# Two of the four block sums of an input projection's pair, moved from a VectorE add to an accumulating DMA

## The chip, the cores and the metric

The kernel runs on one core of a Trainium2 chip. The metric is the device time of one execution in microseconds; the profile is one execution of the same program, taken by the hardware profiler. TensorE does the matrix products, VectorE (DVE in the profile) and ScalarE (ACT) prepare their operands, GpSimd (POOL) does next to nothing before the change, and SyncE (SP) issues nearly all transfers.

## The reference, cut to what matters

One layer of an encoder over 256 tokens of width 4096, all in float32. The two matrices, 4096 x 13312 and 4096 x 4096, are read from HBM once.

```python
h = layer_norm(x, emb_ln_g, emb_ln_b)
p = h @ w_in                    # 256 x 4096 times 4096 x 13312
c_b, c_c, c_h, c_z, a_q, a_k, a_v, a_z = split(p)
y_conv = c_b * centred_short_conv(c_c * c_h, conv_w) * silu(c_z)
y_attn = banded_window_attention(a_q, a_k, a_v, sink) * silu(a_z)
y = concatenate([y_conv, y_attn]) @ w_out
out = layer_norm(2 ** 0.25 * h + y, ln_g, ln_b)
```

## The kernel before

**Steps.** The input projection is cut into 26 chunks of 512 output columns: k, v, then four times (gate z, query q), then four times (c, h, z, b) of the convolution. A chunk is made of steps, which are numbered through from 0; TensorE works them off in order. A single step (a letter `s` in the tables `ORDERS` and `OUT_ORDERS`) is a 1 MB piece of weights, four blocks of 128 rows by 512 columns, and 24 matmuls of 512 columns. A pair step (`S`) covers two such row blocks (512 KB) with a seven-product scheme in the manner of Strassen: it forms sums of quarter blocks, and 21 matmuls of 256 columns take the place of 24. All chunks after k and v have the order `sSsSSsSsSSs`: five singles and six pairs. The input projection has 24 x 6 = 144 pairs, kind `pair`; the output projection has 16 more, kind `opair`.

**A pair's blocks.** A weight buffer is a tile of 128 x 2048 float32, eight blocks of 256 columns. The load fills blocks 0 to 3 (b12, b22, b11, b21). `sums` then makes four more on VectorE: blocks 4 and 5 are blocks 1 and 2 plus block 0, in one instruction of 512 columns (L178); block 6 is block 5 plus block 1 (L179); block 7 is block 6 plus block 3 (L180). Seven blocks, 1 to 7, go on.

**Two halves.** Each step's weights are split into a high part, a copy rounded to float32r on ScalarE (`split_hi`, L197, tile `whi`), and a low part, the difference, on VectorE (`split_lo`, L201, tile `wlo`). TensorE takes three products per operand pair: high times high, high times low, low times high.

**What sets the order.** The order is written out by hand. While TensorE works step j, ScalarE is told to split step j+3, then come the pieces of attention or convolution that are due at j, then `loads(j)` on SP's queue, `sums(j+4)` on VectorE, and `split_lo(j+3)` on VectorE:

```python
        mm_pair(j) if kind == "pair" else mm(j)
        split_hi(j + 3)
...
        loads(j)
        sums(j + 4)
        split_lo(j + 3)
```

Every engine runs its list strictly in order, so the low part of step j+3 stands behind the sums of step j+4.

**The weight buffers.** A load goes into the buffer whose last user is oldest, and it waits until that user's low part is done. There are three buffers `w0` to `w2` and up to three further ones in tiles that are free at the time (`extra`): through most of the attention one more (`w6`), and from the convolution on three more. Between, while the tile of `w6` holds a chunk's sums, there are only the three, which the main loop writes as follows; z0 is 126, the first step of the convolution's first gate chunk, so this holds from step 108 to step 132:

```python
        if j == z0 - 18:
            extra.clear()
        if j == z0 + 6:
            extra.insert(0, (pw, "w6"))
```

With n buffers, the load of step k waits for the low part of step k-n.

Of the kernel before, what the change touches and what calls it, by code (L numbers as in the profile page):

```python
# [11 lines left out]
ALU = mybir.AluOpType  # L12
AX = mybir.AxisListType

P = 128
# [25 lines left out]
HW = W // 2  # L41
# [48 lines left out]
ALL_PAIRS = [u[1:] for u in IN_STEPS + OUT_STEPS if u[0] in ("pair", "opair")]  # L90
# [4 lines left out]
def encoder_kernel(ctx: ExitStack, tc: tile.TileContext, x, emb_g, emb_b, wi, ws, conv_w, sink, wo, ln_g, ln_b, out):  # L95
    nc = tc.nc
# [14 lines left out]
    steps = IN_STEPS + OUT_STEPS  # L111
# [12 lines left out]
    def w_bufs(j):  # L124

        bs = [(wpool, f"w{k}") for k in range(N_W)] + (extra if j < N_IN else [])
        if j >= N_IN and R is not None:
            late = j > in_R[0][0]
            bs += [(None, name) for last, name in in_R if j <= last and late == (name == "R2")]
        last_user = lambda b: max(u for c, u in user.items() if c == b or b[1] == "R2" and c[0] is None) if (  # L130
            b in user or b[1] == "R2") else -1
        return min((last_user(b), k) for k, b in enumerate(bs)), bs

    def load(j, to=None):
        kind, a, b = steps[j]
        if to is None:
            (_, k), bs = w_bufs(j)
            pool, name = bs[k]
            user[bs[k]] = j
            if pool is None:  # L140
                to = raw[j] = {"R0": R[:, 0, D // 2:D], "R1": R[:, 1, D // 2:D], "R2": R[:, :, 3 * D // 4:D]}[name]
            else:
                to = raw[j] = pool.tile([P, PIECE], F32, name=name, bufs=1)
        src = wi[IN_PIECES.index((a, b))] if kind == "in" else wo[OUT_PIECES.index((a, b))] if kind == "out" else None
        if len(to.shape) == 3:
            if is_pair(j):
                nc.sync.dma_start(out=to[:, 0, :], in_=ws[ALL_PAIRS.index((a, b))])
            else:
                nc.sync.dma_start(out=to, in_=src.rearrange("p (i n) -> p i n", i=2))
        elif is_pair(j):  # L150
            nc.sync.dma_start(out=to[:, 0:4 * HW], in_=ws[ALL_PAIRS.index((a, b))])
        else:
            nc.sync.dma_start(out=to, in_=src)

    def loads(j):

        nonlocal nxt
        while nxt < len(steps) and nxt <= j + 7:
            (u, _), bs = w_bufs(nxt)
            if u > j + (2 if len(bs) > N_W else 3):  # L160
                break
            load(nxt)
            nxt += 1

    def sums(j):

        if j >= len(steps) or not is_pair(j):
            return
        if len(raw[j].shape) == 3:
            r0, r1 = (raw[j][:, i, :].rearrange("p (b w) -> p b w", w=HW) for i in range(2))  # L170
            r = lambda k: (r1 if k >= 4 else r0)[:, k % 4, :]
            s01 = r1[:, 0:2, :]
            b12, b22 = r0[:, 0:1, :], r0[:, 1:3, :]
        else:
            t = raw[j].rearrange("p (b w) -> p b w", w=HW)
            r = lambda k: t[:, k, :]
            s01, b12, b22 = t[:, 4:6, :], t[:, 0:1, :], t[:, 1:3, :]
        nc.vector.tensor_tensor(s01, b22, b12.to_broadcast([P, 2, HW]), op=ALU.add)  # L178
        nc.vector.tensor_tensor(r(6), r(5), r(1), op=ALU.add)  # L179
        nc.vector.tensor_tensor(r(7), r(6), r(3), op=ALU.add)  # L180

# [99 lines left out]
    with tc.tile_pool(name="pro", bufs=1) as pro:  # L281
# [13 lines left out]
        nc.sync.dma_start(out=g_c, in_=emb_g)  # L295
        nc.sync.dma_start(out=b_c, in_=emb_b)
        load(0, first[0])
        load(1, first[1])
        x_load(1)
        for j in range(2, 4):  # L300
# [34 lines left out]
        pair = {}  # L335
# [426 lines left out]
    for j in range(n_pro, N_IN):  # L762
        kind, ci, q = steps[j]
# [6 lines that stand above are left out]
        for fn, a in later.pop(j, []):  # L770
            fn(*a)
        if kind == "pair" and q == PAIRS[ci] - 1:
            pair_copy(ci)
            at(j + 1, pair_sums, ci)
        if ci == 1 and 2 <= q < 2 + NP:
            x_sums(q - 2, pa.tile([P, 4 * S], F32, name="xs", tag="zT"))
        if steps[j + 1][1] != ci or j == N_IN - 1:
            if ci == c_ch0:
                at(j + 4, open_pc)
            if PAIRS[ci]:  # L780
                at(j + 1, chunk_end, j + 1, ci)
            else:
                chunk_end(j, ci)
# [3 lines that stand above are left out]
# [148 lines left out]
    for n, (c0, w, pk, j0) in enumerate(chunks):  # L935
        us = out_units(n)
        np_ = sum(u[0] == "opair" for u in us)
        for t, (kind, _, q) in enumerate(us):
            j = j0 + t
# [15 lines left out]
            if j == N_IN + 5:  # L955
                res_load(0)
            sums(j + 4)
            if j + 3 < len(steps):
                split_lo(j + 3)
# [85 lines left out]
```

## Time and profile before

Three runs: median 1544.9 us, 1544.02 to 1545.05. The profiled execution took 1545.18 us; its span, from the first to the last instruction, is 1543.4 us, and the granted TensorE clock is 0.996.

| engine | busy us | share of the span | instructions |
|---|---|---|---|
| TensorE, matmuls | 1522.7 | 99% | 8622 |
| VectorE | 1273.3 | 82% | 1454 |
| ScalarE | 754.1 | 49% | 636 |
| GpSimd | 1.3 | 0% | 7 |

The DMA queues moved 312.96 MB, 203 GB/s over the span. In the profile L178 is a line of the kernel, `w<-in_ws` is a pair's load and `w<-in_wi` a single's, since the program's buffer numbers are left out. An arrow in brackets behind an instruction tells what ended the idle time of its engine before it. A matmul's end is modelled, and matmuls overlap, so TensorE's busy share says that it had work, not that it was at its peak.

### The profile page before, as it was taken

The numbers are of one execution on the slowest core, as the hardware profiler recorded it, in microseconds if no ns is written. First come the engines' busy times: TensorE is split into PE (matmuls) and PEld (weight loads), VectorE is DVE, ScalarE is ACT, GpSimd is POOL, SyncE is SP. The second block draws the span as 40 slices with busy tenths as digits, with TensorE's granted clock in tenths as the row PEclk, the third lists the DMA queues.
The fourth block names the chain that finished last, engine by engine and source line by source line (L and its number), as shares of the span: only waits on it lengthen the run. The fifth ranks groups of instructions, "written<-read, shape, count | busy, mean of one in ns | idle before, by whom it ended". The sixth has DMA issues, their size and how long they took to land.

```text
span 1543.4 us, 21052 instructions
## 1 busy us (share of the span) xinstructions
PE 1522.7 (99%) x8622; PEld 1322.6 (86%) x8622; DVE 1273.3 (82%) x1454; ACT 754.1 (49%) x636; POOL 1.3 (0%) x7
## 2 busy tenths in 40 slices
PE   7999999999999999999999999999999999999997
PEld 4888888888888888888888888888888888888896
DVE  8678798888898888898888888888887688888666
ACT  4545556556465554544454445544555444444331
POOL 0000000000000000000000000000000000000000
PEclk9999999999999999999999999999999999999998
DMA  7535554545545456556555555566557655666752
GB/s 300 202 143 201 205 190 170 197 175 185 201 156 188 163 194 234 214 196 209 198 189 195 214 205 193 192 204 217 199 181 280 261 197 212 254 212 225 252 198 109
DMA packets 65951, 312.96 MB, mean 203 GB/s; under 512 B 7904, under 2 KB 11456, under 8 KB 41920
## 3 DMA queue, kind: packets, MB, share of 16 engines
q1 hardware_dynamic: 65280, 310.06, 56.4%
q8 instruction: 67, 1.10, 0.3%
q10 hardware_dynamic: 576, 1.57, 0.3%
q14 instruction: 28, 0.23, 0.0%
HBM read 303.66 MB, written 7.86 MB: 202 GB/s over the span
## 4 chain that ended last, share of the span: by engine, by line
PE 91%; DVE 4%; ACT 2%; issue 2%; DMA 1%; SPq 0%; DVEq 0%; ACTq 0%
PE acc L238 15%; PE acc L240 15%; PE acc L239 14%; PE acc L869 7%; PE acc L871 7%; PE acc L870 7%; PE pacc L263 4%; PE pacc L262 4%; PE pacc L264 4%; PE acc L263 3%; PE acc L262 3%; PE acc L264 3%; DVE wlo L201 2%; ACT whi L197 1%; PE att L470 1%
## 5 line engine op out<-in xcount | busy, mean ns | idle before, releaser
L197 ACT ACTIVATE whi<-w 128x2048 fp32r<-128x2048 f32 (+1 forms) x330 | 600.0, 1818 | 670.8 <-PE acc L240 288.8
L201 DVE TENSOR_TENSOR wlo<-w,whi 128x2048 fp32r<-128x2048 f32 (+1 forms) x330 | 712.1, 2164 | 197.8 <-ACT whi L197 196.0
L238 PE MATMUL acc<-whi,xT 128*128 128x512 f32 x1072 | 424.4, 396 | 0.0
L240 PE MATMUL acc<-whi,xT 128*128 128x512 f32 x1072 | 419.8, 392 | 0.0
L239 PE MATMUL acc<-wlo,xT 128*128 128x512 f32 x1072 | 417.7, 390 | 0.7 <-DVE wlo L201 0.7
L240 PEld LDWEIGHTS acc<-whi,xT 128*128 128x128 f32 x1072 | 201.3, 188 | 46.8
L239 PEld LDWEIGHTS acc<-wlo,xT 128*128 128x128 f32 x1072 | 201.4, 188 | 41.2 <-DVE wlo L201 1.0
L238 PEld LDWEIGHTS acc<-whi,xT 128*128 128x128 f32 x1072 | 201.5, 188 | 37.8
L869 PE MATMUL acc<-whi,xT 128*128 128x512 f32 (+1 forms) x496 | 182.9, 369 | 0.0
L871 PE MATMUL acc<-whi,xT 128*128 128x512 f32 (+1 forms) x496 | 181.8, 366 | 0.0
L870 PE MATMUL acc<-wlo,xT 128*128 128x512 f32 (+1 forms) x496 | 180.5, 364 | 0.0
L178 DVE TENSOR_TENSOR w<-w 128x512 f32<-128x512 f32 x154 | 105.3, 683 | 5.2 <-DMA w<-in_ws 5.2
L871 PEld LDWEIGHTS acc<-whi,xT 128*128 128x128 f32 x496 | 93.0, 188 | 16.8
L870 PEld LDWEIGHTS acc<-wlo,xT 128*128 128x128 f32 x496 | 93.1, 188 | 15.5
L869 PEld LDWEIGHTS acc<-whi,xT 128*128 128x128 f32 x496 | 93.2, 188 | 14.3 <-issue 0.4
L263 PE MATMUL acc<-wlo,xT 128*128 128x256 f32 x320 | 89.4, 279 | 0.0
L262 PE MATMUL acc<-whi,xT 128*128 128x256 f32 x320 | 89.3, 279 | 0.0
L264 PE MATMUL acc<-whi,xT 128*128 128x256 f32 x320 | 89.1, 278 | 0.0
L262 PE MATMUL pacc<-whi,xT 128*128 128x256 f32 x304 | 86.9, 286 | 0.0
L263 PE MATMUL pacc<-wlo,xT 128*128 128x256 f32 x304 | 84.9, 279 | 0.0
L264 PE MATMUL pacc<-whi,xT 128*128 128x256 f32 x304 | 84.7, 279 | 0.0
L263 PE MATMUL pacc<-wlo,SC 128*128 128x256 f32 x288 | 81.0, 281 | 0.0
(222 smaller groups left out, 1868.1 us busy)
## 6 DMA issues: line engine op xcount, KB each, us to landing
w<-in_wi SPq DMA_DIRECT2D x134, 1024.0 KB
w<-in_ws SPq DMA_DIRECT2D x154, 512.0 KB
w<-in_wo SPq DMA_DIRECT2D x43, 1024.0 KB
R<-in_wo SPq DMA_DIRECT2D x13, 1024.0 KB
yl<-yd SPq DMA_DIRECT2D x7, 512.0 KB
xc<-in_x SPq DMA_DIRECT2D x14, 256.0 KB
x<-in_x SPq DMA_DIRECT2D x6, 512.0 KB
R<-in_ws SPq DMA_DIRECT2D x6, 512.0 KB
```

The source lines that it names most:

```text
L178: nc.vector.tensor_tensor(s01, b22, b12.to_broadcast([P, 2, HW]), op=ALU.add)
L197: nc.scalar.activation(part(j, wh[j]), part(j, raw[j]), AF.Copy)
L201: nc.vector.tensor_tensor(part(j, wl[j]), part(j, raw[j]), part(j, wh[j]).bitcast(F32), op=ALU.subtract)
L238: nc.tensor.matmul(a, xh, hk, start=(first and k == 0), stop=False)
L239: nc.tensor.matmul(a, xh, lk, start=False, stop=False)
L240: nc.tensor.matmul(a, xl, hk, start=False, stop=(last and k == PK - 1))
L262: nc.tensor.matmul(o, ah, hi[:, w, :], start=(opens and p == 0), stop=False)
L263: nc.tensor.matmul(o, ah, lo[:, w, :], start=False, stop=False)
L264: nc.tensor.matmul(o, al, hi[:, w, :], start=False, stop=(closes and last))
L869: nc.tensor.matmul(o, yh, hk, start=first, stop=False)
L870: nc.tensor.matmul(o, yh, lk, start=False, stop=False)
L871: nc.tensor.matmul(o, yl, hk, start=False, stop=last)
```

## The change

The host lays out six blocks for each pair in HBM in place of four: b12, b22, b11, b21, and b22 and b11 once more. An input pair's load fills blocks 0 to 5 with them, 768 KB in place of 512. After it has landed, a DMA that is issued from GpSimd's queue reads b12 from HBM twice (a source step of 0) and adds it to blocks 4 and 5 where they stand in SBUF, in pieces of 256 float32. L178 is left out for these pairs. The output projection's pairs keep their load of four blocks and their VectorE add.

```diff
             if is_pair(j):
-                nc.sync.dma_start(out=to[:, 0, :], in_=ws[ALL_PAIRS.index((a, b))])
+                nc.sync.dma_start(out=to[:, 0, :], in_=ws[ALL_PAIRS.index((a, b)), :, 0:4 * HW])
             else:
                 nc.sync.dma_start(out=to, in_=src.rearrange("p (i n) -> p i n", i=2))
+        elif kind == "pair":
+            w = ws[ALL_PAIRS.index((a, b))]
+            nc.sync.dma_start(out=to[:, 0:6 * HW], in_=w)
+            b12 = bass.AP(tensor=w.tensor, offset=w.offset, ap=[[6 * HW, P], [0, 2], [1, HW]])
+            nc.gpsimd.dma_start(out=to[:, 4 * HW:6 * HW].rearrange("p (b w) -> p b w", b=2), in_=b12, accum_op=ALU.add)
         elif is_pair(j):
-            nc.sync.dma_start(out=to[:, 0:4 * HW], in_=ws[ALL_PAIRS.index((a, b))])
+            nc.sync.dma_start(out=to[:, 0:4 * HW], in_=ws[ALL_PAIRS.index((a, b)), :, 0:4 * HW])
...
-        nc.vector.tensor_tensor(s01, b22, b12.to_broadcast([P, 2, HW]), op=ALU.add)
+        if steps[j][0] == "opair":
+            nc.vector.tensor_tensor(s01, b22, b12.to_broadcast([P, 2, HW]), op=ALU.add)
         nc.vector.tensor_tensor(r(6), r(5), r(1), op=ALU.add)
         nc.vector.tensor_tensor(r(7), r(6), r(3), op=ALU.add)
...
+    blocks = ((0, 1), (1, 1), (0, 0), (1, 0), (1, 1), (0, 0))
+    ws = _np.stack([_np.stack([w_of(ci)[2 * p + k, :, h * HW:(h + 1) * HW] for k, h in blocks],
+                              axis=1).reshape(P, 6 * HW) for ci, p in ALL_PAIRS])
```

VectorE's list around the sums of step 121, the second pair of the stretch with three buffers, stood as follows. `w_4681` is the buffer of step 121, `w_4594` that of step 119, `w_4638` that of step 120, a single.

```order
L201 TENSOR_TENSOR wlo<-w_4594,whi 128x1792
L551 TENSOR_TENSOR den<-den,es 128x2
L553 RECIPROCAL rd<-den 128x2
L178 TENSOR_TENSOR w_4681<-w_4681 128x512
L179 TENSOR_TENSOR w_4681<-w_4681 128x256
L180 TENSOR_TENSOR w_4681<-w_4681 128x256
L201 TENSOR_TENSOR wlo<-w_4638,whi 128x2048
L201 TENSOR_TENSOR wlo<-w_4681,whi 128x1792
```

With the change (lines stand 6 or 7 higher and the buffers have other numbers, `w_4682` for step 121) the same place reads:

```order
L207 TENSOR_TENSOR wlo<-w_4595,whi 128x1792
L557 TENSOR_TENSOR den<-den,es 128x2
L559 RECIPROCAL rd<-den 128x2
L185 TENSOR_TENSOR w_4682<-w_4682 128x256
L186 TENSOR_TENSOR w_4682<-w_4682 128x256
L207 TENSOR_TENSOR wlo<-w_4640,whi 128x2048
L207 TENSOR_TENSOR wlo<-w_4682,whi 128x1792
```

One instruction is gone, and nothing else has changed its place: the two adds that are left, and behind them the low part of step 120, now follow the accumulating DMA instead of the load. GpSimd's list, which before held a few constants and one table, has 144 rows of this kind (`w_4553`, `w_4595` and `w_4682` are the pairs 118, 119 and 121):

```order
L154 DMA w_4553<-in_ws 128x2x256
L154 DMA w_4595<-in_ws 128x2x256
L154 DMA w_4682<-in_ws 128x2x256
L154 DMA w_4770<-in_ws 128x2x256
L154 DMA w_4809<-in_ws 128x2x256
```

Each waits for its own load to land, and SP's queue keeps the order of its loads.

More of the change, by code (lines that the diff above doesn't have):

```diff
@@ L1017 @@
     w_of = lambda ci: w_in[:, :, ci] if ci < OUT else w_o[ci - OUT]
-    ws = _np.stack([_np.stack([w_of(ci)[2 * p + k, :, h * HW:(h + 1) * HW] for k, h in ((0, 1), (1, 1), (0, 0), (1, 0))],
-                              axis=1).reshape(P, 4 * HW) for ci, p in ALL_PAIRS])
+    blocks = ((0, 1), (1, 1), (0, 0), (1, 0), (1, 1), (0, 0))
+    ws = _np.stack([_np.stack([w_of(ci)[2 * p + k, :, h * HW:(h + 1) * HW] for k, h in blocks],
+                              axis=1).reshape(P, 6 * HW) for ci, p in ALL_PAIRS])
     arrays = {
```

## The prediction

> **What bounds the kernel now.** First the page's busy shares, then the list of waits, then the chain of waits that ended last.
>
> ```profile
> PE 1522.7 (99%) x8622; PEld 1322.6 (86%) x8622; DVE 1273.3 (82%) x1454; ACT 754.1 (49%) x636; POOL 1.3 (0%) x7
> PE att L374 <- DMA x<-in_x: 8.6, 1, 8.6
> PE att L910 <- DVE t L905: 3.6, 1, 3.6
> PE acc L239 <- DVE wlo L201: 0.7, 1, 0.7
> PE 91%; DVE 4%; ACT 2%; issue 2%; DMA 1%; SPq 0%; DVEq 0%; ACTq 0%
> ```
>
> TensorE has work almost from end to end. Its waits are at the start (8.6 us for x) and in the final norm (3.6). Of the weight preparation it waits once, 0.7 us. So VectorE is busy and not the bound: taking work off it can give back at most that 0.7 us, well below the 0.2% (3.1 us) that a measurement of this kernel can tell from no change. What can move the time is lateness: a pair's sums that come so late that TensorE finds no weights. So the next question is how much room a pair has, stage by stage; the list of SP's transfers and that of VectorE's instructions, in order of time, show it.
>
> ```profile
> 487.35 0.33 SPq L151 DMA_DIRECT2D w<-in_ws  x1
> 495.22 0.68 DVE L178 TENSOR_TENSOR w<-w 128x512 f32<-128x512 f32 x1
> 641.42 0.33 SPq L151 DMA_DIRECT2D w<-in_ws  x1
> 657.75 0.68 DVE L178 TENSOR_TENSOR w<-w 128x512 f32<-128x512 f32 x1
> 541.26 0.33 SPq L151 DMA_DIRECT2D w<-in_ws  x1
> 545.03 0.69 DVE L178 TENSOR_TENSOR w<-w 128x512 f32<-128x512 f32 x1 [0.60 <-DMA w<-in_ws]
> 596.19 0.83 SPq L151 DMA_DIRECT2D w<-in_ws  x2
> 599.53 0.69 DVE L178 TENSOR_TENSOR w<-w 128x512 f32<-128x512 f32 x1 [1.38 <-DMA w<-in_ws]
> DVE w L178 <- DMA w<-in_ws: 5.2, 4, 2.6
> ```
>
> Each two rows are one pair: its load's issue and its first sum. In the convolution 16.3 us lie between (641.42 to 657.75), in the attention with four buffers 7.9 (487.35 to 495.22). In the stretch with three buffers VectorE already waits for the load itself: 545.03 - 541.26 = 3.8 us, and 599.53 - 596.19 = 3.3, are what a 512 KB load needs, 3.5 as a mean. The landing itself leaves no row; these two waits show it. So the room behind a landing is about 12.8 us in the convolution (16.3 - 3.5), 4.4 in the attention, and none at 521 to 606 us.
>
> **The change part by part.** *Removed:* 144 of the adds on L178.
>
> ```profile
> L178 DVE TENSOR_TENSOR w<-w 128x512 f32<-128x512 f32 x154 | 105.3, 683 | 5.2 <-DMA w<-in_ws 5.2
> L179 DVE TENSOR_TENSOR w<-w 128x256 f32<-128x256 f32 x154 | 65.5, 425 | 5.3
> L180 DVE TENSOR_TENSOR w<-w 128x256 f32<-128x256 f32 x154 | 65.5, 425 | 5.3
> L201 DVE TENSOR_TENSOR wlo<-w,whi 128x2048 fp32r<-128x2048 f32 x176 | 402.6, 2288 | 160.3 <-ACT whi L197 160.3
> ```
>
> 144 x 0.683 = 98 us of VectorE, 1273 to about 1175. TensorE does not wait for it, so this gives 0.
>
> *Load of 768 KB in place of 512.* The rate while transfers run comes from the queue's row:
>
> ```profile
> q1 hardware_dynamic: 65280, 310.06, 56.4%
> ```
>
> 310.06 MB in 0.564 x 1543.4 us is 356 GB/s; 262 KB more take 0.7 us, so a pair's load lands after 3.5 + 0.7 = 4.2 us. In total 144 x (0.262 + 0.262) MB = 75 MB more are read; at that rate they are 212 us of transfers, and the share goes from 56 to 70% before anything for the adding itself. That is below full, so I count no loss of rate.
>
> *The accumulating DMA.* It has no row in the trace, and its time from the load's landing to its own landing, call it A, decides everything. From below: the last store of 256 KB, which is one plain pass.
>
> ```profile
> 1538.45 1.09 SPq L923 DMA_DIRECT2D out<-R  x2
> SPq L1040 <- DMA out<-R: 2.9, 2, 2.3
> 561.03 6.10 DMA w<-in_wi
> ```
>
> Both stores were issued by 1538.45 + 1.09 = 1539.54, and SP then waited up to 2.3 us for the landing; so A is at least 2.3. From above: the add reads the old block and writes the sum, so at worst it is two dependent transfers of a pair load's size, 2 x 3.8 = 7.5; a 1 MB load in the busy stretch (the third row, from the chain) took 6.1, so this is no small bound. Below nothing it can't be, since VectorE waits for it. I take 5.5: one pair load's landing, 3.5, plus 2.0, which is half of a second such pass and some for GpSimd's issue, whose price no row shows. Nearer to the upper end, because the pieces are of 1 KB, two reads go with each write, and it shares the engines with the loads.
>
> The Trainium skill, "DMA: Bandwidth & Descriptors", section "Anatomy of one DMA — SWDGE (gpsimd) path", fits a DMA issued from GpSimd as 2.0 us plus bytes over 436 GB/s. For 262 KB that is an estimate of 2.6 us, near my lower bound; by it the sum below would come to about +3. That fit is for plain copies, and no run here shows it yet.
>
> *What waits behind it.* The two adds that are left wait on VectorE, and VectorE runs in order, so the low part of the step before stands behind them. That low part frees the buffer for the load three (or four) steps on. This closes a ring. One turn through a pair: load 4.2, A 5.5, two adds 2 x 0.425 = 0.9 with their hand-off, low part 2.3: 12.9 us, or 7.4 + A. With three buffers a turn advances two steps, since the low part of step k-1 waits on step k's sums and step k's load waited on step k-3's. What these turns take now stands in SP's rows, as each load is issued when the low part before it ends (the first row counts this wait):
>
> ```profile
> SPq L151 <- DVE wlo L201: 539.6, 137, 7.6
> 541.26 0.33 SPq L151 DMA_DIRECT2D w<-in_ws  x1
> 549.63 2.32 SPq L151 DMA_DIRECT2D w<-in_ws  x2
> 556.92 0.33 SPq L153 DMA_DIRECT2D w<-in_wi  x1
> 563.79 0.33 SPq L151 DMA_DIRECT2D w<-in_ws  x1
> 573.64 3.15 SPq L151 DMA_DIRECT2D w<-in_ws  x2
> 582.22 0.33 SPq L153 DMA_DIRECT2D w<-in_wi  x1
> 587.02 0.33 SPq L151 DMA_DIRECT2D w<-in_ws  x1
> 596.19 0.83 SPq L151 DMA_DIRECT2D w<-in_ws  x2
> 603.38 0.33 SPq L151 DMA_DIRECT2D w<-in_ws  x1
> ```
>
> Six turns pass through a pair: 541.26 to 549.63, to 556.92, 563.79 to 573.64, to 582.22, 587.02 to 596.19, to 603.38. They take 8.4 + 7.3 + 9.9 + 8.6 + 9.2 + 7.2 = 50.5 us, and TensorE is full all the while (last rows); the weights of the stretch's last step are ready at 601.06 + 2.28 = 603.3, and TensorE takes them at 605.5, 2.2 us later:
>
> ```profile
> 601.06 2.28 DVE L201 TENSOR_TENSOR wlo<-w,whi 128x2048 fp32r<-128x2048 f32 x1
> 605.48 0.40 PE L238 MATMUL acc<-whi,xT 128*128 128x512 f32 x1
> 521.00:606.00 85.00, 84.86 (x511) 75.04 (x510) 75.02 (x93) 46.27 (x53) 0.00 (x0) 1.00 0.56 199
> 606.00:1160.00 554.00, 554.00 (x3233) 489.06 (x3232) 473.10 (x497) 269.84 (x173) 0.00 (x0) 1.00 0.57 202
> ```
>
> At 12.9 each they take 77.4: **+27 us**. To this comes how the stretch is entered and left. The room at entry is the attention's 4.4 us behind a landing, and A + 0.7 is set against it: at A = 5.5 that is 1.8 late, which the 2.2 us of readiness at the end cover, so nothing is added or taken off. At A = 2.6 the turns lose 6 x 10.0 - 50.5 = 9.5, less 4.4 and 2.2: the +3 above.
>
> *Attention with four buffers.* There a turn is three steps. Two chunks, 22 steps, are one period:
>
> ```profile
> 423.37 1.93 ACT whi L197
> 518.23 1.93 ACT whi L197
> ```
>
> 94.86 / 22 = 4.3 us a step, 12.9 for three: equal to the turn of 7.4 + 5.5. So at A = 5.5 this stage just holds, and above it every turn loses A - 5.5. *Convolution:* A + 0.7 against 12.8 of room: 0. *Output projection:* its pairs load the same 4 KB per partition and keep their adds: 0. GpSimd's 144 issues lie beside other work, since it does nothing else (1.3 us busy, above); without that cover each would be part of A, which is how I count them.
>
> The sum, against the profiled execution: 1545.2 + 27 = **1572 us**. The profile's own time is 0.3 above the runs' median of 1544.9, which changes nothing here.
>
> **The rivals.**
>
> *The add is hidden after all: about 1545.* If A is 2.1 or less, six turns of at most 9.5 are 57, and the 6.5 over 50.5 are covered by the 4.4 of room at entry and the 2.2 of readiness at the end. Place: SP's three-buffer stretch; price: none; it decides between A = 2.1, where nothing is lost, and 2.6, where the loss reaches the 3.1 us of resolution. For it: the 2.3 us store. Against it: that store is one plain pass from a queue without GpSimd.
>
> *The attention becomes bound by the ring as well: about 1626.* With A = 7.5, a turn is 14.9. The three-buffer stretch loses 6 x 14.9 - 50.5 = 39. The four-buffer stretch, steps 17 to 116, has 33 turns, of which I count two thirds through a pair, since six of eleven steps are pairs and a late turn hands its lateness on (an estimate): 22 x (14.9 - 12.9) = 44. Together some 83, less the 2.2 of readiness. For it: 1 KB pieces, GpSimd's issue, transfers that share the 16 engines with loads. Against it: the 256 KB are small.
>
> *The transfers themselves become the limit: 1700 and more.* If A were 10 or more, the turns alone give 6 x 17.4 - 50.5 = 54 and 22 x 4.5 = 99. The room of the convolution would be nearly gone too. Against it: 70% of the engines' time as counted.
>
> *VectorE's relief counts: 1543 to 1544.* It would need TensorE to be held up by VectorE in the middle; the one such row has 0.7 us. That the DMA does not add, or the old add stays, I exclude: the lists above show it gone.
>
> **How the numbers follow.** Forecast (A from 2.6 to 6.2, loss +3 to +45, likeliest +27): 0.58. Hidden: 0.13. Attention bound too (A 6.2 to 9): 0.22. Transfers the limit: 0.04. Relief: 0.03. The range of 8 in 10 leaves out the hidden case and what lies above A of about 7.8: from 1548 (A = 2.6) to 1640. Faster is the relief alone, 0.03; same is 0.13, the hidden case; slower is the rest, 0.84.
>
> **What would show it.** The add of 512 columns (L178, now L184) falls from 160 to the 16 of the output projection, and VectorE to about 1175 us. TensorE's first new idle time lies between 540 and 640 us, before L238 or L239 and put down to the low part (now L207); the same stretch shows VectorE's L185 waiting for the DMA in almost every pair. Loads in that stretch stand about 12.9 us apart per turn. The attention before 520 us loses under 5 us, and the convolution from 640 on runs at the old pace, two chunks in 688.33 - 602.73 = 85.6 us:
>
> ```profile
> 602.73 0.44 PE att L470 x4
> 688.33 0.44 PE att L470 x4
> ```
>
> I am wrong if TensorE's idle time spreads over all of the attention (A larger), if it does not appear (A smaller), or if the convolution slows, which no step of mine allows.

## The result, and the profile after

The changed kernel takes 1676.4 us (median of 4 runs, 1669.87 to 1680.92) beside 1545.0 for the kernel before (4 runs): a ratio of 1.0849, 95% interval 1.0815 to 1.0883. It is slower, as forecast, but by 131 us instead of 27, and the time lies above the range, which ended at 1640. The profiled execution took 1673.9 us with a span of 1672.2 and a granted clock of 0.974; the one before took 1545.18.

First the page of the changed kernel: the busy shares, and the two queues that carry weights (packets, MB, share of 16 engines' span).

```profile
PE 1561.3 (93%) x8622; PEld 1344.4 (80%) x8622; DVE 1176.8 (70%) x1310; ACT 752.2 (45%) x636; POOL 174.7 (10%) x151
PEclk9999999989999999899999999999999999999998
q1 hardware_dynamic: 65280, 347.81, 58.7%
q0 software_dynamic: 39168, 37.76, 15.1%
```

VectorE is relieved by 96.5 us, close to the 98 of the working, and TensorE is idle where it was full before. TensorE's new waits, from the list of waits (engine, tile, line, releaser: us, times, longest):

```profile
PE acc L245 <- DVE wlo L207: 55.2, 23, 5.1
PE att L533 <- DVE qhl L521: 25.7, 4, 7.8
PE att L572 <- DVE s L538: 8.6, 4, 4.6
DVE w L185 <- DMA w<-in_ws: 287.6, 74, 11.5
ACT whi L203 <- DVE w L186: 311.3, 82, 12.1
```

VectorE, which waited 5.2 us in all for a pair's load, now waits 288 for the accumulating DMA, and TensorE waits for what stands behind that on VectorE: the low parts, as the working had it, and also pieces of the attention (L521, L538), which it had not named.

The table by stage shows where. The stretches of the changed kernel are cut at the same matmuls as those of before, so the first number behind the colon can be compared: 130 against 158, 291 against 342, 85 (its row stands in the prediction) against 124, 554 against 564. Before, then after (us, busy time of PE, PEld, DVE, ACT, POOL with counts, granted clock, DMA share, GB/s):

```profile
100.00:230.00 130.00, 129.31 (x741) 113.30 (x740) 110.08 (x127) 65.80 (x48) 0.00 (x0) 1.00 0.52 185
230.00:521.00 291.00, 290.58 (x1758) 257.47 (x1757) 247.49 (x307) 169.94 (x197) 0.00 (x0) 1.00 0.51 181
```

```profile
100.00:258.00 158.00, 138.23 (x741) 118.64 (x740) 98.27 (x109) 64.87 (x48) 20.41 (x17) 0.95 0.72 212
258.00:600.00 342.00, 303.66 (x1753) 264.90 (x1752) 221.66 (x269) 168.19 (x196) 43.32 (x36) 0.95 0.71 209
600.00:724.00 124.00, 97.22 (x514) 82.57 (x513) 66.47 (x79) 46.88 (x55) 14.46 (x12) 0.90 0.63 186
724.00:1288.00 564.00, 557.77 (x3238) 490.52 (x3238) 422.30 (x422) 270.36 (x174) 93.91 (x78) 1.00 0.90 270
```

Some 79 us go in the attention with its four buffers, 39 in the three-buffer stretch, 9 to 10 in the convolution. In the first three the granted clock is below 1 as well. Both kernels issue the same 8622 matmuls in the same order, so they can be laid side by side in the trace, matmul by matmul: of the 128.2 us between the two, 96.8 are 36 places where TensorE stands still (a start over 0.3 us later than before), and 31.8 are 193 matmuls that start up to 0.3 us further apart than before. Of these, 161 matmuls (28.4 us) lie in times at which the trace records half the clock.

The next table has this by stage, cut at the same matmuls, together with the middle (median) landing of that stage's pair loads and of their adds, and the middle time from a pair's load to the end of the low part behind its sums. It is worked out from the matmuls' starts and the semaphore events of the trace, in us.

| stage, by the time before | lost | TensorE still | matmuls slower | load lands after | add lands after | load to release |
|---|---|---|---|---|---|---|
| attention, 100 to 230 | 27.8 | 20.8 | 7.7 | 5.3 | 5.7 | 15.2 |
| attention, 230 to 521 | 51.6 | 40.0 | 11.5 | 5.6 | 6.5 | 15.9 |
| three buffers, 521 to 606 | 39.1 | 29.0 | 10.1 | 4.4 | 4.7 | 14.0 |
| convolution, 606 to 1160 | 8.9 | 7.0 | 2.1 | 6.2 | 7.7 | 19.5 |

One turn of the ring in the attention, from the timelines of SP, GpSimd and VectorE (start, duration, what it waited for):

```profile
311.85 0.33 SPq L152 DMA_DIRECT2D w<-in_ws  x1
...
317.48 1.20 POOL L154 DMA_DIRECT2D w<-in_ws  x1 [12.17 <-DMA w<-in_ws]
...
325.42 0.42 DVE L185 TENSOR_TENSOR w<-w 128x256 f32<-128x256 f32 x1 [6.73 <-DMA w<-in_ws]
325.87 0.42 DVE L186 TENSOR_TENSOR w<-w 128x256 f32<-128x256 f32 x1
326.22 2.28 DVE L207 TENSOR_TENSOR wlo<-w,whi 128x2048 fp32r<-128x2048 f32 x1
```

The load and GpSimd's waking take 5.6 us (311.85 to 317.48), the add 7.9 (to 325.42), the two VectorE adds and the low part 3.1 (to 328.50): 16.7 us from a load to the release of the next buffer, where three steps of a full TensorE last 12.9. Over all 144 adds, issue to landing was, in the view of that line:

```profile
DMA to landing us min/median/max: 4.1/7.0/11.9
```

The load's landings, by the semaphore events of the trace, start at 4.1 us and have a median of 5.85; GpSimd wakes 0.56 us behind them. So in the prediction's terms A is 4.7 us at the least and about 7.5 in the middle of all pairs. That middle leans to the convolution, which has over half of them; by the table A is 6.3 and 7.1 in the attention and 5.3 in the three-buffer stretch.

The six turns of the three-buffer stretch that the prediction read off SP's rows look as follows after the change:

```profile
630.34 0.33 SPq L152 DMA_DIRECT2D w<-in_ws  x1
644.11 2.26 SPq L152 DMA_DIRECT2D w<-in_ws  x2
656.85 0.33 SPq L158 DMA_DIRECT2D w<-in_wi  x1
662.10 0.33 SPq L152 DMA_DIRECT2D w<-in_ws  x1
677.19 2.86 SPq L152 DMA_DIRECT2D w<-in_ws  x2
690.07 0.33 SPq L158 DMA_DIRECT2D w<-in_wi  x1
694.00 0.33 SPq L152 DMA_DIRECT2D w<-in_ws  x1
707.08 0.82 SPq L152 DMA_DIRECT2D w<-in_ws  x2
723.68 0.33 SPq L152 DMA_DIRECT2D w<-in_ws  x1
```

They take 13.8 + 12.7 + 15.1 + 12.9 + 13.1 + 16.6 = 84.2 us, where 50.5 were taken before and 77.4 forecast.

### The profile page after: what moved, and what is told of

Same layout as the page of the kernel before. It is cut to its first block, busy times and chain, and to the rows that moved or that the text cites. A ratio compares the mean times of both kernels' runs of the same rounds, so it can differ in the third digit from the quotient of the medians.

```text
span 1672.2 us, 21438 instructions
## 1 busy us (share of the span) xinstructions
PE 1561.3 (93%) x8622; PEld 1344.4 (80%) x8622; DVE 1176.8 (70%) x1310; ACT 752.2 (45%) x636; POOL 174.7 (10%) x151
## 3 DMA queue, kind: packets, MB, share of 16 engines
q0 software_dynamic: 39168, 37.76, 15.1%
## 4 chain that ended last, share of the span: by engine, by line
PE 48%; DMA 9%; DVE 5%; issue 1%; ACT 0%; SPq 0%; DVEq 0%; POOLq 0%; ACTq 0%
DMA w<-in_ws 9%; PE acc L875 6%; PE acc L877 6%; PE acc L876 6%; PE acc L245 6%; PE acc L246 6%; PE acc L244 6%; DVE wlo L207 3%; PE pacc L268 2%; PE pacc L269 2%; PE pacc L270 2%; PE acc L269 2%; PE acc L268 2%; PE acc L270 2%; DVE w L185 0%
## 5 line engine op out<-in xcount | busy, mean ns | idle before, releaser
L245 PE MATMUL acc<-wlo,xT 128*128 128x512 f32 x1072 | 432.5, 403 | 55.3 <-DVE wlo L207 55.2
L244 PE MATMUL acc<-whi,xT 128*128 128x512 f32 x1072 | 434.2, 405 | 0.0
L246 PE MATMUL acc<-whi,xT 128*128 128x512 f32 x1072 | 429.2, 400 | 0.0
L245 PEld LDWEIGHTS acc<-wlo,xT 128*128 128x128 f32 x1072 | 207.9, 194 | 105.6 <-DVE wlo L207 63.8
L154 POOL DMA_DIRECT2D w<-in_ws x144 | 173.4, 1204 | 1036.8 <-DMA w<-in_ws 635.0
L185 DVE TENSOR_TENSOR w<-w 128x256 f32<-128x256 f32 x154 | 65.0, 422 | 288.1 <-DMA w<-in_ws 287.6
L246 PEld LDWEIGHTS acc<-whi,xT 128*128 128x128 f32 x1072 | 208.0, 194 | 47.5
L244 PEld LDWEIGHTS acc<-whi,xT 128*128 128x128 f32 x1072 | 208.4, 194 | 41.5
L877 PEld LDWEIGHTS acc<-whi,xT 128*128 128x128 f32 x496 | 93.3, 188 | 16.8
L876 PEld LDWEIGHTS acc<-wlo,xT 128*128 128x128 f32 x496 | 93.2, 188 | 15.7
L875 PEld LDWEIGHTS acc<-whi,xT 128*128 128x128 f32 x496 | 93.3, 188 | 14.9 <-issue 0.4
```

Of the source, the lines that this page charges most:

```text
L154: nc.gpsimd.dma_start(out=to[:, 4 * HW:6 * HW].rearrange("p (b w) -> p b w", b=2), in_=b12, accum_op=ALU.add)
L244: nc.tensor.matmul(a, xh, hk, start=(first and k == 0), stop=False)
L245: nc.tensor.matmul(a, xh, lk, start=False, stop=False)
L246: nc.tensor.matmul(a, xl, hk, start=False, stop=(last and k == PK - 1))
L875: nc.tensor.matmul(o, yh, hk, start=first, stop=False)
L876: nc.tensor.matmul(o, yh, lk, start=False, stop=False)
```

## The experiments

What has to be told apart: is the loss the *ring* (VectorE, in order, stands waiting for a landing, and low parts and attention stand behind it), or the *traffic* (the extra bytes and the read-modify-write on the shared transfer engines, wherever anyone waits)? And is the loss in the stretch that the prediction named?

**The larger load alone.** Six blocks are loaded, nothing is added by DMA, and VectorE's old add stays:

```diff
-            nc.gpsimd.dma_start(out=to[:, 4 * HW:6 * HW].rearrange("p (b w) -> p b w", b=2), in_=b12, accum_op=ALU.add)
...
-        if steps[j][0] == "opair":
+        if True:
             nc.vector.tensor_tensor(s01, b22, b12.to_broadcast([P, 2, HW]), op=ALU.add)
```

> The load of six blocks is kept, the accumulating DMA is left out, and VectorE does its add of 512 columns as before. Ring theory (the loss comes from VectorE waiting for an add that lands late): a load that lands 0.7 us later is covered by the room of 2.2 us before TensorE, so 1545 to 1548. Traffic theory (the loss comes from the bytes that are moved more): half of the 75 MB are here, so a good part of the 129 us, above 1580.

Measured: 1544.9 us (10 runs), ratio 0.9997 (0.9988 to 1.0006). 37.75 MB more cost nothing that can be seen.

**The traffic without the wait.** To that, 144 accumulating DMAs of the same shape into a scratch tensor in HBM, each behind its pair's load; nobody waits for them:

```diff
...
+            nc.gpsimd.tensor_copy(tick, to[:, 0:1])
+            nc.gpsimd.dma_start(out=scr.rearrange("p (b w) -> p b w", b=2), in_=b12, accum_op=ALU.add)
```

> As x1_load6, and with 144 accumulating DMAs of the same size, pieces and source, each issued when its load has landed, but into scratch rows in HBM that nobody reads; VectorE does its own add and waits only for the load. Ring theory: the loads share the engines and land after about 5.8 us instead of 4.3, a turn without the add is 5.8 + 1.6 + 2.3 = 9.7 us against 8.4 in the three-buffer stretch, six turns lose 8, of which 6.6 of room are covered: 1545 to 1552. Traffic theory: the whole traffic is here, so most of the loss, above 1620.

Measured: 1555.1 us (4 runs), ratio 1.0060 (1.0044 to 1.0077). These adds land as late as those of the changed kernel:

```profile
DMA to landing us min/median/max: 4.3/6.6/11.4
```

They keep the 16 transfer engines busy for 0.172 x 1553.4 = 267 us, where the changed kernel's took 252. 6.8 of the 9.5 us that its profile lost fall into the three-buffer stretch, where VectorE waits for loads anyway. So traffic alone is about 10 us of 131, some 3 more than the ring theory allowed for; the adds' destination is HBM here, not SBUF, which is the limit of this run.

**Stage by stage.** Two kernels make some pairs by DMA and the rest by VectorE: only from step 138 on (the convolution), and all but steps 112 to 137 (the three-buffer stretch).

```diff
+    by_dma = lambda j: steps[j][0] == "pair" and (j >= 138)
```

> Accumulating DMAs only for the pairs of step 138 on, in the convolution; all earlier pairs load four blocks and are added by VectorE. Ring theory: room of 12.8 us behind a landing covers the 7 of the add and the 1.6 by which loads land later, so 1545 to 1554 (the changed kernel lost 8.9 us in this stage, part of it inherited). Traffic theory: 78 of 144 adds, about half of the loss, 1600 or more.

```diff
+    by_dma = lambda j: steps[j][0] == "pair" and (not 112 <= j < 138)
```

> All pairs by DMA but those of steps 112 to 137, the stretch with three buffers and what follows it. If each stage pays for itself, the 39 us that the stretch lost come back, and the attention's 79 and the convolution's 9 stay: about 1635. If the three-buffer stretch is the place, as the prediction had it, and the attention was late only through it, 1550 to 1565.

Measured: 1557.6 us (7 runs), ratio 1.0086 (1.0056 to 1.0116), for the convolution alone, 4 us above the ring theory's 1554; 1640.2 (2 runs), 1.0616 (1.0594 to 1.0637), with the three-buffer stretch spared. The second one's table by stage, cut at the matmuls that stood at 230, 521 and 606 us before:

```profile
264.00:609.00 345.00, 306.99 (x1759) 267.08 (x1758) 225.41 (x274) 170.32 (x199) 40.91 (x34) 0.94 0.69 205
609.00:694.00 85.00, 84.86 (x510) 75.04 (x509) 74.67 (x92) 46.22 (x53) 0.00 (x0) 1.00 0.58 201
```

The spared stretch is back at 85 us and TensorE is full in it, while the attention ahead of it still loses its time (33.8 us up to the matmul of 230, 53.9 from there to that of 521). Each stage pays for itself. The prediction's place was a real one, worth 36 to 39 us, but not the main one.

**The low part ahead of the sums.** If the ring is closed because the low part of step j+3 stands behind the sums of j+4, then exchanging the two opens it:

```diff
         loads(j)
-        sums(j + 4)
         split_lo(j + 3)
+        sums(j + 4)
```

> The changed kernel with one exchange: the low part of step j+3 is issued on VectorE ahead of the sums of step j+4, so no low part stands behind another step's late add. Ring theory: a turn then goes through the step's own parts, load 5.8, add 7, sums 0.9, high part 1.7, low part 2.0 = 17.4 us, but for as many steps as there are buffers: four steps take 17.2, so the attention about holds, three take 12.9, and some five turns of the three-buffer stretch lose 4.5 each; with the convolution's 9 and the slow matmuls after stalls 1570 to 1600. If the order on VectorE is not what matters and the add's landing alone sets the pace, 1660 to 1680 as before.

Measured: 1631.1 us (4 runs), ratio 1.0527 (1.0489 to 1.0564): 45 us better than the changed kernel, and still 85 lost, between what the two theories expected. The waits show where the time goes now:

```profile
ACT whi L203 <- DVE w L186: 432.0, 106, 11.3
DVE wlo L207 <- ACT whi L203: 307.8, 198, 3.4
DVE w L185 <- DMA w<-in_ws: 91.2, 31, 7.8
```

VectorE waits less for the DMA (91 us against 288) and more for ScalarE (308 against 150). A low part needs the high part of its step, and that needs the sums. The exchange takes VectorE's stall apart but puts the high part, 1.8 us, into the same pair's way to its low part, as the expectation had it. What the expectation had too small is the sum: it left out GpSimd's waking and took the low part at 2.0. With this run's own medians in the attention, load 5.6 to 5.9, waking 0.6, add 6.4 to 6.8, two adds 0.9, high part 1.8 and low part 2.3 are 17.6 to 18.3 us, to be done in four steps of TensorE (17.2 us); in the three-buffer stretch (load 5.0, add 5.8) they are 16.4, to be done in three (12.9). That is an account fitted afterwards; it gives both stages a loss, as measured (58 us up to 521, 20 in the three-buffer stretch).

**A plain copy in place of the add.** The GpSimd DMA copies b12 into the two blocks instead of adding it; the sums are not formed:

```diff
-            nc.gpsimd.dma_start(out=to[:, 4 * HW:6 * HW].rearrange("p (b w) -> p b w", b=2), in_=b12, accum_op=ALU.add)
+            nc.gpsimd.dma_start(out=to[:, 4 * HW:6 * HW].rearrange("p (b w) -> p b w", b=2), in_=b12)
```

> The DMA from GpSimd copies the two blocks over the old ones instead of adding (the sums are then not formed, so the output is not the reference's). Everything else is the changed kernel. A piece should take about 46 ns instead of 102, so each engine is busy 0.7 us less with one DMA. If the reading and writing of the old block is what stretches the transfers, 1600 to 1620; if issuing from GpSimd and waiting on it is the price, 1655 to 1675.

Measured: 1594.5 us (2 runs), ratio 1.0314 (1.0293 to 1.0335), below what either reading expected. The same bytes from HBM, the same place in the program, another operation on the way:

```profile
q1 hardware_dynamic: 65280, 347.81, 60.7%
q0 software_dynamic: 11520, 37.76, 7.0%
```

```profile
DMA to landing us min/median/max: 3.0/4.2/7.2
```

The copies keep the 16 transfer engines busy for 0.070 x 1592.1 = 111 us, the adds for 0.151 x 1672.2 = 252, and they land after 4.2 us in the middle, not 7.0. One more thing differs: by the packet records the copy moves 64 packets of 4 KB and the add 256 of 1 KB. That is the smaller part: a 1 KB packet took 46 ns in the middle as a plain load in the kernel before and 102 as an add, and a 4 KB one of the copy 159, that is 40 for each KB. So most of the difference is the adding and not the size of the pieces. Even so 49 us are lost: a plain transfer between the load and VectorE's add is already too long for the ring.

**Half the bytes, and who reads them.** A first run has the DMA make block 4 alone; VectorE makes block 5, and the load is of five blocks.

```diff
-            nc.sync.dma_start(out=to[:, 0:6 * HW], in_=w)
+            nc.sync.dma_start(out=to[:, 0:5 * HW], in_=w[:, 0:5 * HW])
...
+            nc.gpsimd.dma_start(out=to[:, 4 * HW:5 * HW], in_=b12, accum_op=ALU.add)
...
+        else:
+            nc.vector.tensor_tensor(r(5), r(2), r(0), op=ALU.add)
```

> The DMA adds to one block only (128 pieces of 1 KB), a pair's load brings five blocks, and VectorE makes the other sum (256 columns, 0.43 us). If transfers that share the engines stretch load and add (5.8 for 4.3 and 7 for 4.7), half the adding takes off more than its own 0.8 us: load 4.9, add 5.3, sums 1.3, low part 2.3 = 13.8 a turn: three-buffer stretch 26, attention 20, slow matmuls and the convolution 14: about 1605. If the add's time is its fixed part, a turn is 15.1 and the time 1640 to 1660.

Measured: 1557.0 us (2 runs), ratio 1.0072 (1.0051 to 1.0092), far better than either theory had it. The run had changed two things at once, which I saw only then: half the bytes, and also the wait. Block 6 is made from block 5, block 7 from block 6, and no VectorE add reads block 4, so none of VectorE's adds waits for the DMA any more; only ScalarE's high part does, and the low part behind it. Two further runs take this apart. Both load all six blocks and add 128 KB by DMA; one adds block 5, which VectorE's next add reads, the other block 4, which it doesn't.

```diff
+            nc.gpsimd.dma_start(out=to[:, 5 * HW:6 * HW], in_=b12, accum_op=ALU.add)
...
+        else:
+            nc.vector.tensor_tensor(r(4), r(1), r(0), op=ALU.add)
```

> The load of six blocks stays; the DMA adds only block 5, which VectorE's next add reads, and VectorE itself makes block 4 with one add that needs the load alone. So 128 KB are added instead of 256, and VectorE still waits for the landing inside the ring. Ring theory: landing of the add about 4.3 us as in the copy of the same size range, turn = load 4.5 + wake 0.6 + 4.3 + two adds 0.9 + low part 2.3 = 12.6 us, at the limit of the four-buffer attention and far above the three-buffer stretch's 8.4: about +45 us like the plain copy, 1580 to 1600 us. Rival, the loss goes with the bytes that are added and with where the engines are shared: the same as the half add on the other block, about 1557 us.

```diff
+            nc.gpsimd.dma_start(out=to[:, 4 * HW:5 * HW], in_=b12, accum_op=ALU.add)
...
+        else:
+            nc.vector.tensor_tensor(r(5), r(2), r(0), op=ALU.add)
```

> As the run beside it, with the same bytes, but the DMA adds block 4, which no add of VectorE reads (only the two parts that ScalarE and VectorE make of the whole pair), and VectorE makes block 5. Ring theory: VectorE waits for the load only, the turn is 4.5 + three adds 1.3 + low part 2.3 = 8.1 us, inside the 8.4 of the three-buffer stretch; what is left is ScalarE's wait for block 4: 1550 to 1562 us. Rival (bytes alone): the same as the run beside it, within 5 us.

Measured: 1613.6 us (4 runs), ratio 1.0435 (1.0408 to 1.0462), where VectorE waits; 1558.9 (4 runs), 1.0085 (1.0057 to 1.0113), where it does not. First the one that waits, then the other:

```profile
DVE w L187 <- DMA w<-in_ws: 127.4, 44, 7.5
DMA to landing us min/median/max: 2.9/4.4/10.3
```

```profile
ACT whi L205 <- DMA w<-in_ws: 64.5, 17, 8.2
DMA to landing us min/median/max: 2.9/4.6/9.5
```

The same bytes, landing as late (4.4 and 4.6 us in the middle): 55 us between the two hang on who waits. The first one's loss, 68 us, is above the 35 to 55 expected.

**The whole add, VectorE not waiting.** The DMA adds both blocks as in the changed kernel, and VectorE makes block 6 from three loaded blocks, one add more per pair:

```diff
+            nc.vector.tensor_tensor(r(6), r(5), r(1), op=ALU.add)
+        else:
+            nc.vector.tensor_tensor(r(6), r(0), r(1), op=ALU.add)
+            nc.vector.tensor_tensor(r(6), r(6), r(2), op=ALU.add)
```

> The DMA adds both blocks as in the changed kernel, but VectorE makes the third block from three loaded ones (two adds for one: block 6 = 0 + 1, then + 2), so that none of its adds waits for the accumulating DMA; ScalarE's high part and VectorE's low part still need it, and VectorE has 61 us more to do. Ring theory: the traffic is the changed kernel's (about +10 us as in the scratch run), the turn on VectorE is 5.8 + 1.3 + 2.3 = 9.4 us: 1555 to 1585 us. Rival, the loss is the late blocks and the shared engines wherever the wait stands: above 1640 us.

Measured: 1586.4 us (4 runs), ratio 1.0253 (1.0233 to 1.0274), 1.4 us above what the ring theory expected. The adds land as late as ever, and the waiting has moved to ScalarE:

```profile
ACT whi L206 <- DMA w<-in_ws: 161.8, 38, 10.4
DMA to landing us min/median/max: 4.1/6.9/14.0
```

90 of the 131 us went with VectorE's wait, although VectorE has more to do. 41 stay. About 10 of them are what the scratch run lost by traffic; the rest I put down to the longer way load, add, high part, low part (5.7 + 0.6 + 6.9 + 1.8 + 2.3 = 17.3 us against 17.2 with four buffers and 12.9 with three). No run separates these two, and the sum does not hold stage by stage: with this run's medians up to the matmul of 230 (load 6.0, add 4.9) it is 15.6, below 17.2, and 12.5 us are lost there all the same.

**Stalls alone.** The kernel before, with 6 to 20 extra VectorE adds ahead of one low part at eleven steps of the convolution, so that TensorE is held up for chosen lengths, with no change to any transfer:

```diff
...
+        for _ in range({140: 6, 151: 8, 162: 9, 173: 10, 184: 11, 195: 12, 206: 13, 217: 14, 228: 15, 239: 17, 250: 20}.get(j, 0)):
+            nc.vector.tensor_tensor(late, tab, tab, op=ALU.add)
```

> The kernel before, with no accumulating DMA; at eleven steps of the convolution, 11 steps apart, VectorE gets 6 to 20 additional adds of 512 columns (0.68 us each) ahead of a low part, so that TensorE stalls there once. The room before TensorE is about 4 us and some idle time, so stalls of about 0 to 9 us. If TensorE's clock falls after a stall that is long enough (about 3 us in the changed kernel's trace), the stalls under 2.8 us are followed by at most 0.1 us of slow matmuls and the longer ones by 1.5 to 2.7 us at a start-to-start time of 0.427 us for 0.229. If the slow matmuls came from the transfers or from GpSimd, there are none here.

Measured: 1614.2 us (one run, no interval). 51.1 us of its loss are TensorE standing still and 18.1 are slower matmuls. The 4 us right behind a hold-up of 2.3 us (734.8), of 2.2 (781.9) and of 5.2 (925.1), and the last one once more some 7 us on:

```profile
737.10:741.10 4.00, 3.86 (x21) 3.73 (x22) 3.93 (x6) 1.70 (x1) 0.00 (x0) 0.67 0.38 131
...
784.50:788.50 4.00, 3.14 (x23) 2.77 (x23) 3.90 (x6) 2.42 (x3) 0.00 (x0) 1.00 0.38 131
...
930.70:934.70 4.00, 4.00 (x20) 4.00 (x21) 3.93 (x5) 1.70 (x1) 0.00 (x0) 0.50 0.42 133
938.00:942.00 4.00, 4.00 (x23) 3.43 (x22) 1.57 (x1) 0.64 (x1) 0.00 (x0) 1.00 0.81 238
```

Behind every hold-up of 3.6 us and more (seven of them, 3.6 to 10.3) the clock was granted at half for 3.4 to 6.1 us of TensorE's work, which cost 1.6 to 2.9 us each; behind those of 2.2 us and less it was not; the one of 2.3 cost 1.65. Length alone does not decide: in the run with the plain copy a hold-up of 3.7 us (at 159 us) passed with nothing behind it.

The traces' records of the granted clock show why. In each trace the clock changes only on a grid of 3.41 us (here 738.46, 741.88, 834.03, 837.45 and so on). TensorE's 2.16 us of idle time in the hold-up of 2.3 (735.08 to 737.24) lay inside one step of the grid and filled 63% of it, and half clock came with the next step; in the plain copy's run the idle time from 159.63 to 163.17 lay across a step's end at 161.53, filled 56% of one step and 48% of the next, and the clock stayed full. So it counts how much of one step stands idle. In the traces of the changed kernel and of ten of the experiments, away from the start and the end, every step at full clock that was 62% idle or more (59 of them) was followed by half clock, none that was 50% idle or less was, and between the two it went both ways.

So the slower matmuls of the changed kernel, as far as they lie at half clock (28.4 of 31.8 us), are a consequence of its stalls, and need no cause in the transfers.

The Trainium skill, "TensorE: Matmul & The Clock Gate", section "HAM oscillation — how this bites in real kernels", says that the array falls to half its clock after idle gaps above about 3.4 us. The seven hold-ups of 3.6 us and more agree; the one of 2.3 us shows that less can be enough, and the plain copy's of 3.7 us that more need not be.

The runs that change every pair, in one table; the last column is the median less that of the kernel before beside it.

| kernel | VectorE waits for the DMA | us | ratio | loss |
|---|---|---|---|---|
| changed kernel | yes, 256 KB | 1676.4 | 1.0849 | 131 |
| low part ahead of the sums | yes, less | 1631.1 | 1.0527 | 85 |
| half, block 5 | yes, 128 KB | 1613.6 | 1.0435 | 68 |
| plain copy | yes, 256 KB copied | 1594.5 | 1.0314 | 49 |
| whole add, block 6 made apart | no, 256 KB | 1586.4 | 1.0253 | 41 |
| half, block 4 | no, 128 KB | 1558.9 | 1.0085 | 14 |
| half, block 4, load of five | no, 128 KB | 1557.0 | 1.0072 | 11 |
| add into scratch | nobody waits | 1555.1 | 1.0060 | 10 |
| six-block load alone | no add | 1544.9 | 0.9997 | 0 |

None beats the kernel before, in which TensorE is busy from end to end and VectorE's add costs it nothing.

## Why the prediction was wrong in size

Put side by side, the prediction's 27 us are 27 of standing still in the three-buffer stretch and nothing elsewhere. Measured were 29 of standing still there, 61 in the attention, 7 in the convolution, and 32 us of matmuls slowed, mostly at half clock. So the forecast term was right, and two terms set to nothing were the loss: the attention and the clock.

**Right.** VectorE's relief is worth nothing to TensorE: 96.5 us came off and none of it reached the end. The larger load is free. The ring is the mechanism: a landing put between a load and VectorE's next add, in an engine that works in order, holds back the low part that frees the next buffer. In the place that the prediction priced, its numbers were close: load 4.4 for 4.2, A 5.3 for 5.5, six turns 84.2 us for 77.4, 29 us of standing still for 27. Of the runs with the same bytes, those where VectorE waits lose 55 us (half) and 90 us (whole) more than those where it doesn't. The output projection loses 0.8 us, as good as the 0 predicted.

**Step 1 that failed: "That is below full, so I count no loss of rate."** The prediction counted the adds as 38 MB more at 356 GB/s, 106 us, and "before anything for the adding itself". The adding itself kept the engines busy for 252 us, 2.4 times that and 2.3 times a plain copy. In the convolution the share rose from 0.57 to 0.90. And it need not be full to cost time: the six-block load landed after 4.3 us in the middle with no adds (the first run above), 5.7 with adds into scratch and 5.85 in the changed kernel. In the attention, where the share was 0.71 to 0.72, it was 5.3 to 5.6, so there the first term of the turn was 1.1 to 1.4 us too small.

The Trainium skill, "DMA: Bandwidth & Descriptors", section "Issuing engines are not separate DMA queues", says that transfers of all issuing engines run on the same 16 DMA engines and interleave. The loads' landings, 1.5 us later than the 4.3 that they take with no adds among them, agree with it.

**Step 2: A = 5.5.** One value was used for all stages, and A is not one value. The fastest adds took 4.1 and 0.6 for waking, 4.7 in all; in the three-buffer stretch, where the transfers' share is lowest (0.63), the middle is 5.3, in the attention 6.3 and 7.1, in the convolution 8.3. The prediction reasoned its way to the value from undisturbed transfers, though it named the sharing as a reason to go higher. Its upper bound, 7.5, was the middle of all pairs, not the end of the range (11.9 + 0.6).

The prediction's page for the GpSimd path ("DMA: Bandwidth & Descriptors", "Anatomy of one DMA — SWDGE (gpsimd) path", of the Trainium skill) gave an estimate of 2.6 us for 256 KB. The plain copy took 3.0 at the least and 4.2 in the middle, the add 4.1 and 7.0; for this kernel the formula is too low by 0.4 even for the fastest copy.

**Step 3: "at A = 5.5 this stage just holds".** The attention was put on a knife's edge by equal numbers, 12.9 and 12.9, and its loss set to 0. With the attention's medians a turn is 5.3 + 6.3 + 0.9 + 2.3 = 14.8 us up to the matmul of 230 and 5.6 + 7.1 + 0.9 + 2.3 = 15.9 behind it (load to release, measured, 15.2 and 15.9), so the attention cannot hold. With the load that no add disturbs and the fastest add, a turn is 4.3 + 4.7 + 0.9 + 2.3 = 12.2 and would have held. That the difference is the transfers' sharing is shown for the loads (4.3, and 5.7 with adds into scratch); for the adds it is argued, since no run has them without loads. This was the rival "The attention becomes bound by the ring as well", 1626 at A = 7.5, to which I gave 0.22. Its mechanism was the right one. Its price for the three-buffer stretch, 39, equals the 39.1 measured there, but that is luck: it stood for turns of 14.9 with TensorE standing still, and measured were turns of 14.0, 29.0 us of standing still and 10.1 of slower matmuls. For the attention it gave 44 where 79 were lost.

**Step 4, a term that was missing: TensorE's clock.** Every stage was priced as time in which TensorE stands still. Of the attention's 79 us about 61 are that, and 19 are slower matmuls, mostly at half clock behind a stall; over the whole kernel 97 and 32. The rival's 44 stands against those 61. Its turns were too short: at the 15.7 that the attention's pairs took in the middle (15.2 and 15.9, weighted by 18 and 36 pairs), its 22 turns come to 22 x 2.8 = 62. That is an estimate, as the count of 22 is; no run checks the count.

**Step 5, behind the waiting instruction.** The prediction named the low part as what stands behind the waiting adds. The attention's own pieces stand there too, and TensorE waited 25.7 and 8.6 us for them (L521, L538), 34 of its 90 us of new waits.

**Step 6: the convolution.** "A + 0.7 against 12.8 of room: 0". It lost 9 us in the changed kernel, and the run with DMA adds only from step 138 on lost 12 (1.0086); in its profile 4.4 us of that are in the convolution, up to the matmul that stood at 1160 before, and 4.0 behind it. There the share is highest and the adds land latest, 7.3 us in the middle of its first half and 8.6 in that of its second, up to 11.9. The room of 16.3 us from a load to the first sum covers the middle (6.2 + 0.6 + 7.7) and not the end. The trace shows that the late adds are what stalls it, here in its longest stop (GpSimd, VectorE, TensorE):

```profile
823.15 1.20 POOL L154 DMA_DIRECT2D w<-in_ws  x1 [7.03 <-DMA w<-in_ws]
...
834.27 0.43 DVE L185 TENSOR_TENSOR w<-w 128x256 f32<-128x256 f32 x1 [6.75 <-DMA w<-in_ws]
...
835.07 2.29 DVE L207 TENSOR_TENSOR wlo<-w,whi 128x2048 fp32r<-128x2048 f32 x1
...
837.41 0.50 PE L245 MATMUL acc<-wlo,xT 128*128 128x512 f32 x1 [2.28 <-DVE wlo L207]
```

All five stops of TensorE in this stage (2.3, 0.9, 1.6, 0.7 and 0.7 us) end in this way, behind adds that took 9.7 to 11.1 us. Other adds as late passed without a stop.

**What would have shown it, and did.** The prediction said it would be wrong "if TensorE's idle time spreads over all of the attention (A larger)", and "if the convolution slows, which no step of mine allows". Both happened. So did a third: TensorE's first new idle time was to lie between 540 and 640 us, and its first new stop ends at 135 us, in the attention.

## What to carry to other kernels

When an operation of an in-order engine is moved to a DMA, ask first which instruction waits for the landing and what stands behind it on that engine: here the same 128 KB cost 14 us where no VectorE add read the result and 68 where the next one did. Price the landing with the traffic that it will meet, its own included, and with a read-modify-write at more than twice a copy's engine time; when a stage's verdict is a tie between two sums, price it as lost. Take landings stage by stage: the middle of all adds, 7.0 us, is that of no stage where the loss arose (5.7, 6.5 and 4.7). And to a stall of TensorE of some 3 us or more add about 2 us at half clock (1.6 to 2.9 here).

## What was not expected of the hardware

- An accumulating DMA of 256 KB in 1 KB pieces took 4.1 us from issue to landing at best, 7.0 in the middle and 11.9 at worst; the plain copy, in 4 KB pieces, 3.0, 4.2 and 7.2. It kept the transfer engines busy 2.3 times as long (252 against 111 us for 144 of them); a 1 KB piece took 102 ns as an add and 46 as a plain load.
- GpSimd was busy for 1.20 us to issue one (0.72 for the plain copy, 0.86 for half the bytes), and woke 0.56 us after the load's landing.
- 37.75 MB of additional loads in plain large pieces moved the time by nothing (ratio 0.9997, 0.9988 to 1.0006), and the same amount of accumulating traffic into HBM that nobody waits for, on top of them, by 10 us.
- The half clock came back to full 3.4 to 6.1 us after TensorE resumed, and one hold-up of only 2.3 us brought it on. The changes of the clock lay on a grid of 3.41 us.
